# Second parts of eleven ring weights: subtraction on GpSimd instead of VectorE

## The chip, the core and the metric

The kernel runs on one core of a Trainium2 chip. The engines are TensorE (PE in the profile; its weight loads stand apart as PEld), VectorE (DVE), ScalarE (ACT), GpSimd (POOL) and SyncE (SP), which issues most of the DMAs. Each engine works through its own queue in the order written when the program is built; semaphores join them. The metric is the device time of one execution in microseconds. Before the change it is 1038.24 us, the median of three runs.

## The reference

One layer of a decoder, for a prompt of 512 tokens and eight samples of four tokens, 544 columns in all. Each layer normalises, projects, mixes in two ways in parallel (sparse attention, and a convolution), projects again, and then does a gated feed-forward block. The part that matters here is the convolution module and the input projection:

```python
def mixer_prompt(u, lp):
    q5, kv6, g3, conv_in, ga, gb = split_projection(u, lp['w_in'])
    ...
    hist = jnp.pad(conv_in, ((0, 0), (CONV_W - 1, 0), (0, 0)))
    o_conv = conformer_conv(hist, lp)
    y = merge_out(o_nsa, o_conv, ga, gb, lp['w_out'])

def conformer_conv(hist, lp):
    y = lax.conv_general_dilated(hist, lp['w_dw'][:, None, :], window_strides=(1,), padding='VALID',
                                 dimension_numbers=('NWC', 'WIO', 'NWC'),
                                 feature_group_count=C_CONV) + lp['b_dw']
    y = jax.nn.silu(layer_norm(y, lp['ln_conv_g'], lp['ln_conv_b']))
    return jnp.einsum('btc,cd->btd', y, lp['w_pw2'])
```

`split_projection` multiplies the normalised input by `w_in` (1024 rows); its columns are the queries, six key and value blocks, the branch gates, the gated conv input (`glu`) and the two merge gates. The convolution is depthwise: 31 taps on each of 512 channels, then a layer norm over the channels.

## The kernel before

**Two-part products.** The kernel keeps fp32 accuracy on TensorE by splitting each operand into two parts of a reduced fp32 form (`F32R`): a first part `h`, which ScalarE makes by a copy (`hi`, line 168), and a second part `l = raw - h`, which is a subtraction of two SBUF tensors (`lo`, line 171, on VectorE unless an engine is given). `zmm` multiplies a weight tile of 128 output columns: 16 matmuls with the first part `wh` (against both parts `hh` and `hl` of the input), and then 8 with the second part `wl`. A tile is done in two halves of 272 columns (`zhalf`, `ztile`), each with 24 matmuls; so `wl` is needed 16 matmuls after `wh`.

**The ring.** All weights stream through one ordered list, `RING`. Each entry has a time on the program's clock, a kind and a number: `(76.104, "kv", 0)`. The clock is a sorting key by which the body emits its work (an event heap, `ev`, `spawn`, `run`); it is not the time on the chip. In the stretch of the change the entries are `glu` (projection for the conv input), `kv` (twelve tiles of keys and values), `g` (branch gates), and between them `ada` and `qs` entries, which TensorE uses as they are loaded (`is_raw`). The raw weights of 512 KB go into tile `wraw`, of which there are three buffers (`NB`), and every second `ada` entry from 17 on into `xraw`, which has one. `load_more` emits a load as soon as the program's count has a buffer for it; on the chip SP's DMA waits until the last reader of the buffer it takes is done: the matmuls for a raw entry, `hi` and `lo` for a split one. SP issues loads in the planned order, so a load that waits holds those behind it.

**Splitting.** `split_upto` makes `wh` and `wl` of an entry; there are two buffers of each. `take` splits the entry that is asked for and, if it is near, the next one too. `ada_part` and `q_sample` call `split_upto` after a raw entry, so that the following tile is ready ahead of its matmuls.

**VectorE's other work there.** `conv` (line 685 on) runs the depthwise convolution, one `scalar_tensor_tensor` of 128x512 per tap (line 711), for four channel groups of 31 taps. The samples' taps are one product on GpSimd (`cpr`, line 702) and a reduction on VectorE (line 703). `layer_norm` first sends the conv state out by two DMAs of GpSimd (lines 715 and 716), adds the four groups (`lacc`, lines 719 to 721) and has TensorE sum over the channels; the products for `pw2` follow. The gated conv input `hist` and `hst` is written by VectorE (lines 678 to 682), and GpSimd's product and its output DMAs wait for that.

**The order.** The body's emission order gives the priority of each instruction. The framework then plans the order on each engine, and the buffer of each tile, with modelled costs, when the program is built; the chip follows that order.

**ScalarE around kv 7.** ScalarE's queue holds, in this order, the first part of kv 7 (line 168), a copy of keys out of PSUM (line 781), the copies for the compressed blocks (`Xc`, line 824) and `qz` (line 905), from which TensorE makes the samples' queries.

Of the kernel before, what the change touches and what calls it, by code (L numbers as in the profile page):

```python
# [79 lines left out]
def _plan():  # L80

    p = [(1 + 0.1 * n, "glu", n) for n in range(NG)]
    p += [(2.345 + 0.089 * n, "ada", n) for n in range(8, 12)]
    p += [(45.047 + 6.5 * (n - NG), "glu", n) for n in range(NG, 8)]
    p += [(76.104 + 10.023 * n, "kv", n) for n in range(12)]
    p += [(60.955 + 4.999 * n, "ada", 16 + n) for n in range(16)]
    p += [(at(3, 1.557 + 0.388 * n), "ada", 32 + n) for n in range(16)]
    p += [(164.548, "g", 0)]
    p += [(203.02 + 3.438 * n, "pw2", n) for n in range(8)]
    p += [(114.735 + 9.994 * n, "qs", n) for n in range(8)]  # L90
    p += [(TA + 6.676 * n, "q", n) for n in range(2)]
    for g in range(4):
        if g < 3:
            p += [(at(g, 6.173 if g == 0 else 5.336), "q", 2 * g + 2), (at(g, 9.783) - 1.608, "q", 2 * g + 3)]
        p += [(at(g, 12.132 + 0.267 * n) if g < 3 else at(3, 0.308 + 0.745 * n), "ga", 2 * g + n) for n in range(2)]
    for n, (g, x) in enumerate(((0, 1.6), (0, 3.4), (0, 4.8), (0, 8.0), (1, 4.5), (1, 7.7), (2, 4.5), (2, 7.7))):
        p += [(at(g, x), "gb", n)]
    p += [(TO + 3.069 * n, "out0", n) for n in range(8)]
    p += [(TO + 31.9 + 2.718 * n, "out1", n) for n in range(5)]
    p += [(TO + 50.404 + 3 * NF * hf + 2.986 * n, "fi%d" % hf, n) for hf in range(2) for n in range(NF)]  # L100
    p += [(TS + 0.008 * n, "sf", n) for n in range(NF, 44)]
    p += [(TG + 64.062 * hf + 7.662 * ft + 3.08 * kg, "fo%d" % hf, fo_entry(ft, kg))
          for hf in range(2) for ft in range(8) for kg in range(3)]
    return [(t + 1e-4 * i, kind, n) for i, (t, kind, n) in enumerate(sorted(p))]


RING = _plan()
# [5 lines left out]
def body(ctx, tc, xT, cT, cst, sel, vecs, b1row, wall, w1, pool_rows, kwin, vwin, convst, ptab,  # L113
# [53 lines left out]
    def hi(dst, src, scale=1.0):  # L167
        act.activation(dst, src, AF.Copy, scale=scale)  # L168

    def lo(dst, src, h, eng=None):  # L170
        (eng or dve).tensor_sub(dst, src, h.bitcast(F32))  # L171
# [17 lines left out]


    NB = 3
    def is_raw(j):
        _, kind, n = RING[j]
        return kind in ("ada", "qs", "sf") or kind == "glu" and n < NG
# [22 lines left out]
    def load_more(end=len(RING)):  # L217

        while rst["load"] < end:
            j = rst["load"]  # L220
            _, kind, n = RING[j]
            own = kind == "ada" and 15 < n < 32 and n % 2
            pl, tag, bufs = (xr, "xraw", 1) if own else (wp, "wraw", NB)
            if j < 4 + NG and j % 3:
# [19 lines left out]
    def split_upto(i):  # L244
        while rst["split"] <= min(i, len(RING) - 1):
            j = rst["split"]
            rst["split"] = j + 1
            if is_raw(j):
                continue
            raw, k, tag = raws.pop(j)  # L250
            out[tag] -= 1
            own = RING[j][1] == "out0" and RING[j][2] in KEPT
            h, l = ((kp if own else wp).tile([128, 1024], F32R, name=w, tag=w, bufs=3 if own else 2) for w in ("wh", "wl"))
            hi(h[:, :k], raw[:, :k])
            m = 640 if RING[j][1] in () else k
            lo(l[:, :m], raw[:, :m], h[:, :m])
            if m < k:
                lo(l[:, m:k], raw[:, m:k], h[:, m:k], pool)
            splits[j] = h.rearrange("p (k m) -> p k m", m=128), l.rearrange("p (k m) -> p k m", m=128)

    def take(kind, n):

        i = rst["use"]
        rst["use"] = i + 1
        assert RING[i][1:] == (kind, n), (RING[i], kind, n)
        if is_raw(i):
            return raws.pop(i)[::2]
        split_upto(i)
        j = i + 1
        while j < len(RING) and is_raw(j):  # L270
            j += 1
        if j - i <= NB - 1:
            split_upto(j)
        load_more()
        return splits.pop(i)
# [63 lines left out]
    def ada_part(part, bank):  # L339

        def step(k):
            raw, tag = take("ada", 8 * part + k)
            if k == 0:
                ada_ps[part] = bank()
            ada_product(ada_ps[part], k, raw)
            raw_done(tag)
            split_upto(rst["use"])
            if k == 7:
                z = ada_quarters(ada_ps.pop(part))
                ev(when("ada", 8 * part + 7) + 4.968, turn, z)  # L350

        def turn(z):
            dve.tensor_add(adaT[:, part].rearrange("p (q a) b -> p a q b", a=2), ada_turned(z)[1],
                           ada_bias(part)[:, :, :, None].to_broadcast([128, 2, 4, 9]))

        for k in range(8):
            ev(when("ada", 8 * part + k), step, k)
# [115 lines left out]
    with tc.tile_pool(name="p0", bufs=1) as p0:  # L473
# [44 lines left out]
        for f in range(NG):  # L518
            h = p0.tile([128, 8, 128], F32R, name="w0h", tag="w0h", bufs=NG)
            l = p0.tile([128, 8, 128], F32R, name="w0l", tag="w0l", bufs=NG)  # L520
            w0s.append((h, l))
            raw, tag = take("glu", f)
            raw = raw.rearrange("p (k m) -> p k m", k=8)
# [1038 lines left out]
    raw, split, bank, keep = {}, {}, {}, {}  # L1562
# [273 lines left out]
```

## Time and profile before

| what | us |
| --- | --- |
| median of three runs | 1038.24 |
| lowest and highest of them | 1037.79, 1039.67 |
| the profiled execution's own time | 1035.17 |
| its span, first to last instruction | 1033.3 |
| PE busy in it | 1006.7 |
| VectorE busy | 730.8 |
| ScalarE busy | 529.4 |
| GpSimd busy | 130.8 |

The profile is of one execution. A row of the timeline gives start, length, engine, line, operation, output and inputs, shapes and a count; in brackets stands how long the engine was idle before it and what ended that. A row of the chain of waits gives start, length and the instruction that the end of the program hung on. A window row gives the busy time of each engine in a stretch, then the granted TensorE clock, the DMA engines' busy share and the rate in GB/s. A wait row gives who waited for whom, the total, how often, and the longest. Times in rows are counted from the first instruction.

### The profile page before, as it was taken

The numbers are of one execution on the slowest core, as the hardware profiler recorded it, in microseconds if no ns is written. First come the engines' busy times: TensorE is split into PE (matmuls) and PEld (weight loads), VectorE is DVE, ScalarE is ACT, GpSimd is POOL, SyncE is SP. The second block draws the span as 40 slices with busy tenths as digits, with TensorE's granted clock in tenths as the row PEclk, the third lists the DMA queues.
The fourth block names the chain that finished last, engine by engine and source line by source line (L and its number), as shares of the span: only waits on it lengthen the run. The fifth ranks groups of instructions, "written<-read, shape, count | busy, mean of one in ns | idle before, by whom it ended". The sixth has DMA issues, their size and how long they took to land.

```text
span 1033.3 us, 21219 instructions
## 1 busy us (share of the span) xinstructions
PE 1006.7 (97%) x8488; PEld 908.3 (88%) x8488; DVE 730.8 (71%) x1356; ACT 529.4 (51%) x1174; POOL 130.8 (13%) x142
## 2 busy tenths in 40 slices
PE   9998999999999999999998999999999999999996
PEld 7898899999877777777874799999999999999996
DVE  5689996343675775766757748899888988544554
ACT  5332125465546456454535556756666666444442
POOL 0040100001244244243231000000000000000000
PEclk9999999999999999999999999999999999999998
DMA  9955865424344343424436454654323233555652
GB/s 353 392 162 198 286 196 175 146 79 142 140 144 161 106 144 125 161 83 157 150 124 203 144 209 134 219 165 142 112 93 104 101 101 105 210 175 183 203 177 84
DMA packets 52195, 167.57 MB, mean 162 GB/s; under 512 B 6224, under 2 KB 8672, under 8 KB 51712
## 3 DMA queue, kind: packets, MB, share of 16 engines
q1 hardware_dynamic: 41328, 131.38, 38.0%
q10 hardware_dynamic: 7056, 20.81, 5.6%
q0 software_dynamic: 3712, 14.02, 4.1%
q8 instruction: 67, 1.10, 0.4%
q14 instruction: 32, 0.26, 0.1%
HBM read 149.38 MB, written 16.81 MB: 161 GB/s over the span
## 4 chain that ended last, share of the span: by engine, by line
PE 84%; DMA 6%; DVE 5%; ACT 2%; issue 1%; SPq 0%; DVEq 0%; ACTq 0%
PE mm L165 51%; PE pv L165 11%; PE big L165 10%; PE pt L165 5%; DMA wraw<-in_wall_dram 4%; PE big L1138 3%; DVE cy L711 2%; PE big L609 1%; DMA first<-in_wall_dram 1%; DMA xraw<-in_wall_dram 1%; DVE wl L171 1%; PE mm L609 1%; DMA x<-in_xT_dram 1%; ACT Xc L824 1%; PE pv L538 0%
## 5 line engine op out<-in xcount | busy, mean ns | idle before, releaser
L171 DVE TENSOR_TENSOR wl<-wraw,wh 128x1024 fp32r<-128x1024 f32 (+1 forms) x135 | 156.3, 1159 | 130.8 <-ACT wh L168 116.3
L168 ACT ACTIVATE wh<-wraw 128x1024 fp32r<-128x1024 f32 (+1 forms) x183 | 166.0, 908 | 155.8 <-PE mm L165 94.3
L165 PE MATMUL mm<-hh,wh 128*128 128x272 f32 (+1 forms) x608 | 172.7, 311 | 0.5 <-ACT at L671 0.5
L165 PE MATMUL mm<-hl,wh 128*128 128x272 f32 (+1 forms) x608 | 167.4, 302 | 0.0
L165 PEld LDWEIGHTS mm<-hh,wh 128*128 128x128 f32 x608 | 116.1, 191 | 12.9 <-issue 5.9
L165 PEld LDWEIGHTS mm<-hl,wh 128*128 128x128 f32 x608 | 115.6, 190 | 5.8 <-issue 2.8
L165 PE MATMUL mm<-hh,wl 128*128 128x272 f32 (+1 forms) x608 | 100.4, 302 | 2.7 <-DVE wl L171 2.7
L165 PEld LDWEIGHTS mm<-hh,wl 128*128 128x128 f32 x608 | 85.4, 189 | 8.6 <-issue 3.0
L1110 ACT ACTIVATE PB<-big,mx 128x128 f32<-128x128 f32 (+3 forms) x128 | 66.1, 526 | 51.0 <-DVE mx L1107 45.9
L165 PE MATMUL mm<-uh,wh 128*128 128x272 f32 x352 | 90.2, 289 | 1.0 <-ACT wh L168 1.0
L165 PE MATMUL mm<-ul,wh 128*128 128x272 f32 x352 | 90.1, 288 | 0.0
L711 DVE SCALAR_TENSOR_TENSOR cy<-hist,vc,cy 128x512 f32<-128x512 f32 x120 | 88.6, 791 | 0.4
L165 PE MATMUL mm<-h2h,wh 128*128 128x272 f32 x328 | 77.4, 288 | 0.0
L1118 POOL TENSOR_SCALAR PB<-PB,mx 128x128 f32<-128x128 f32 (+3 forms) x56 | 60.7, 1099 | 78.2 <-DVE mx L1115 34.1
L165 PEld LDWEIGHTS mm<-uh,wh 128*128 128x128 f32 x352 | 66.4, 189 | 1.2 <-ACT wh L168 1.2
L165 PE MATMUL mm<-h2l,wh 128*128 128x272 f32 x260 | 66.6, 287 | 0.0
L165 PEld LDWEIGHTS mm<-ul,wh 128*128 128x128 f32 x352 | 66.2, 188 | 0.0
L165 PEld LDWEIGHTS mm<-h2h,wh 128*128 128x128 f32 x328 | 58.5, 188 | 0.0
L165 PE MATMUL mm<-h2h,wl 128*128 128x272 f32 x312 | 53.1, 288 | 0.5 <-ACT pv L1605 0.5
L165 PE MATMUL mm<-uh,wl 128*128 128x272 f32 x352 | 52.2, 288 | 0.0
L1107 DVE TENSOR_REDUCE mx<-big 128x2 f32<-128x256 f32 (+3 forms) x64 | 51.0, 816 | 0.5
L165 PEld LDWEIGHTS mm<-h2l,wh 128*128 128x128 f32 x260 | 48.9, 188 | 0.0
(489 smaller groups left out, 2212.0 us busy)
## 6 DMA issues: line engine op xcount, KB each, us to landing
wraw<-in_wall_dram SPq DMA_DIRECT2D x170, 512.0 KB, 4.2
X<-in_rows_dram SPq DMA_DIRECT2D x32, 256.0 KB, 5.0
wraw<-in_wall_dram SPq DMA_DIRECT2D x16, 384.0 KB, 3.7
first<-in_wall_dram SPq DMA_DIRECT2D x8, 512.0 KB, 10.2
xraw<-in_wall_dram SPq DMA_DIRECT2D x8, 512.0 KB, 6.5
kw<-in_kwin_dram ACTq DMA_DIRECT2D x8, 512.0 KB, 3.5
out_wk_dram<-kw ACTq DMA_DIRECT2D x8, 512.0 KB, 5.2
vw<-in_vwin_dram ACTq DMA_DIRECT2D x8, 512.0 KB, 3.5
```

The source lines that it names most:

```text
L165: pe.matmul(out, lhsT, rhs, start=start, stop=stop, **more)
L168: act.activation(dst, src, AF.Copy, scale=scale)
L171: (eng or dve).tensor_sub(dst, src, h.bitcast(F32))
L609: ins = pe.matmul(gl[f][hf][:, :HT], w[:, k], r[:, k, sl], start=k == 0 and part == 0, stop=k == 7 and part == 2).ins
L711: dve.scalar_tensor_tensor(y, hist[:, ct, k:k + TP], w, y, op0=OP.mult, op1=OP.add)
L824: act.activation(o, src[:, r], AF.Copy)
L1107: dve.tensor_reduce(mx[:, 0, r, 2 * jj:2 * jj + 2], sc[:, :, :w], axis=AX.X, op=OP.max, negate=True)
L1110: act.activation(P[r][:, :, j * 128:j * 128 + 128], sc[:, jp, :w].rearrange("p (k n) -> p k n", n=128), AF.Exp, bias=mx[:, 0, r, j:j + 1], ...
L1118: (dve if r or g == 3 and i > 1 else pool).tensor_scalar(v, v, m[:, j:j + 1], None, op0=OP.mult)
L1138: pe.transpose(p[:, x, j * 128:j * 128 + 128], P[r][:, kt, j * 128:j * 128 + 128], ident)
```

## The change

The second part of a ring weight whose clock lies strictly between 68 and 165 is worked out by GpSimd, all 1024 columns of it. The entries are glu 7, kv 0 to 8 and g; raw entries have no second part. All other weights keep VectorE. The first parts, the matmuls and the loads are written as they were.

```diff
@@ -189,6 +189,8 @@
     NB = 3
+    A_LO, B_LO = 68, 165
+
     def is_raw(j):
@@ -252,8 +254,9 @@
             hi(h[:, :k], raw[:, :k])
-            m = 640 if RING[j][1] in () else k
-            lo(l[:, :m], raw[:, :m], h[:, :m])
+            m = 0 if A_LO < RING[j][0] < B_LO else k
+            if m:
+                lo(l[:, :m], raw[:, :m], h[:, :m])
             if m < k:
                 lo(l[:, m:k], raw[:, m:k], h[:, m:k], pool)
```

## The prediction

> **What bounds the kernel now.** I read the page first, then the groups of the moved line, the waits of PE, the chain of waits in the stretch of the change, and the timelines of POOL, ACT and PE there.
>
> ```profile
> span 1033.3 us, 21219 instructions
> PE 1006.7 (97%) x8488; PEld 908.3 (88%) x8488; DVE 730.8 (71%) x1356; ACT 529.4 (51%) x1174; POOL 130.8 (13%) x142
> 86.00:112.00 26.00, 26.00 (x227) 23.62 (x227) 26.00 (x35) 5.01 (x12) 3.88 (x4) 1.00 0.67 222
> 170.00:190.00 20.00, 19.93 (x182) 18.68 (x181) 5.03 (x6) 13.48 (x35) 0.00 (x0) 1.00 0.46 160
> ```
>
> TensorE is busy for 97% of the span. In the windows (columns: stretch, length, then busy time of PE, PEld, DVE, ACT, POOL) both PE and DVE are full from 86 to 112 us; from 170 to 190 PE still is (19.93 of 20) and DVE is three quarters idle. Two full engines side by side do not say which one sets the end. The moved line does:
>
> ```profile
> L171 DVE TENSOR_TENSOR wl<-wraw,wh x11: 1205/1226/1226, 89.5 to 182.7; 128x1024 fp32r<-128x1024 f32 x11
> its engine sat idle before it (us, times) until:
>   ACT wh L168: 8.8, 6
> who waited for it (us, times):
> ```
>
> ```profile
> PE mm L165 <- DVE wl L171: 2.7, 1, 2.7
> 118.73 0.64 PE L165 MATMUL big<-xraw,cs 128*32 128x256 f32 x8 [1.84 <-DMA xraw<-in_wall_dram]
> 82.11 1.21 DVE L171 TENSOR_TENSOR wl<-wraw,wh 128x1024 fp32r<-128x1024 f32 x1
> ```
>
> The change moves eleven ring entries: glu 7 (clock 71.05), kv 0 to 8 (76.1 to 156.3) and g (164.55). In the order of the ring they are these eleven subtractions, from 89.5 to 182.7 us, and under "who waited" stands nothing: no compute engine waited for any of them. The second fence has PE's wait on a `wl` and two timeline rows. Between 60 and 240 us PE waits on a `wl` once, for 2.7 us, and that one runs at 82.11 us. It belongs to glu 6, whose clock is 64.55, below 68; it stays on VectorE, and all that stands ahead of it is unchanged. So VectorE is relieved where PE does not wait for it.
>
> Someone else does wait for these subtractions: the next load. A `wraw` buffer is free only when the subtraction has read it, and SP issues the next DMA then.
>
> ```profile
> SPq L236 <- DVE wl L171: 21.7, 8, 5.9
> SPq L236 <- PE big L165: 18.3, 9, 7.1
> 160.25 1.07 ACT wh L168
> 161.34 1.24 DVE wl L171
> 163.01 6.12 DMA wraw<-in_wall_dram
> 169.22 1.06 ACT wh L168
> 178.78 0.29 ACT qz L905
> 179.12 0.41 PE pt L165 x2
> ```
>
> The first two rows are SP's waits between 84 and 190 us, for VectorE and for PE; the others are the chain of waits. In this stretch the chain leaves PE: ScalarE's first part of kv 6 (160.25), its second part on VectorE (161.34), the load issued by SP behind that (163.01), the first part of kv 7 (169.22), then ScalarE's queue without a pause until `qz` at 178.78, ended at 179.07, and `qz`'s product on PE at 179.12. PE idles for 0.07 us in these twenty (above), so it was done just as `qz` was: its slack there is under 0.1 us, I take 0.05, and what is late on this chain is late on PE.
>
> **The change part by part.** Removed from VectorE: 11 x 1.21 us = 13.3 us, and nothing of the span, because nobody on PE waits. Added on GpSimd: 11 subtractions of 128x1024 with both inputs in SBUF. The trace has none of that form; the nearest rows are these:
>
> ```profile
> L702 POOL TENSOR_TENSOR cpr<-hst,vc 128x992 f32<-128x992 f32 x4 | 9.9, 2487 | 21.5 <-issue 14.6 <-DVE cy L703 5.4 <-DMA hst<-in_conv_dram 1.6
> L1020 POOL TENSOR_TENSOR m<-m,O 128x272 f32<-128x272 f32 x6 | 4.6, 774 | 15.0 <-DVE O L1018 8.4 <-DVE mx L1115 6.6
> 83.87 2.56 POOL L702 TENSOR_TENSOR cpr<-hst,vc 128x992 f32<-128x992 f32 x1 [14.58 <-issue]
> 83.67 3.31 DVE L711 SCALAR_TENSOR_TENSOR cy<-hist,vc,cy 128x512 f32<-128x512 f32 x2
> 150.29 6.71 DVE L711 SCALAR_TENSOR_TENSOR cy<-hist,vc,cy 128x512 f32<-128x512 f32 x10
> ```
>
> The product at line 702 is almost the same size and runs beside conv taps: 2.49 us, times 1024/992 = 2.57 us. I take 2.55 us. The upper end is the sum of line 1020 in proportion, 774 ns x 1024/272 = 2.9 us; the lower one is the time for which VectorE is held (next paragraph), 2.0 us.
>
> The last three rows show what GpSimd costs VectorE. Ten taps alone take 6.71 us, 0.67 each; the two taps beside GpSimd's product take 3.31 instead of 1.34 us, 1.97 more. So each move takes 1.14 us off VectorE (1.21 less the overlap with the next start) and puts some 1.9 us back as blocked time: VectorE gets not shorter but 0.75 us longer per entry. After glu 7 and kv 0 to 3 it is about 3.8 us late, and then it stays so, since its pauses before the six later subtractions (8.8 us, above) go too.
>
> The Trainium skill, GPSIMD Engine Reference, section "3.1 Elementwise — side-by-side cycle accounting", gives 4497 ns for such an operation at 2048 elements; half of it, as an estimate, is 2.25 us, and with it the sum below would be +1.7 instead of +2.5 us.
>
> VectorE's lateness costs nothing as long as the layer norm has room:
>
> ```profile
> 168.77 0.72 DVE L721 TENSOR_TENSOR lacc<-lacc,cy 128x544 f32<-128x544 f32 x1
> 189.47 0.62 PE L165 MATMUL pt<-lacc,c 128*128 128x272 f32 x2
> ```
>
> The last sum after the taps ends at 169.5, its product stands at 189.5 in PE's order. That room of 20 us is also why a faster VectorE could win nothing. Its price if the room were gone is up to 3.8 us.
>
> Now the path that sets the end, the loads behind kv 4 to kv 7:
>
> ```profile
> 149.95 0.22 PE big L165 x4
> 148.06 1.06 ACT L168 ACTIVATE wh<-wraw 128x1024 fp32r<-128x1024 f32 x1 [4.55 <-DMA wraw<-in_wall_dram]
> 149.15 1.23 DVE L171 TENSOR_TENSOR wl<-wraw,wh 128x1024 fp32r<-128x1024 f32 x1 [1.22 <-ACT wh L168]
> 150.41 0.84 SPq L236 DMA_DIRECT2D wraw<-in_wall_dram  x2
> 153.08 1.18 PE L165 MATMUL mm<-hh,wl 128*128 128x272 f32 x8
> 162.42 0.39 PE L165 MATMUL mm<-hh,wh 128*128 128x272 f32 x1
> 164.54 1.18 PE L165 MATMUL mm<-hh,wl 128*128 128x272 f32 x8
> ```
>
> From kv 4 on VectorE stands idle when the first part is done, so the second part ends 1.26 us after it (148.06 + 1.06 to 150.38); on GpSimd 2.55: +1.3 us each time, and each time SP's next burst of four loads starts behind it, in order.
> - kv 4: its burst's first load is 1.3 us later, but the later ones wait for PE anyway (9 such waits, above) and follow at SP's pace of 0.4 us: kv 5's load, the fourth, lands between +0.4 (one step of SP) and +1.3; I take +0.7.
> - kv 5: 0.7 + 1.3 = +2.0. Its second part is ready at 152.4, needed at 153.08: no wait. But the burst of 150.41 starts 2.0 us later, and kv 6's first part is ready at 163.3 instead of 161.3, needed at 162.42: PE waits about 0.9.
> - kv 6: +3.3 us; its second part is ready at 165.9, with PE at 164.54 + 0.9: 0.4 us more. The burst behind it starts 3.3 us later, and so do kv 7's first part and ScalarE's queue up to `qz`. PE loses 3.3 in all at 179 us (the 1.3 already lost is within it).
> - Against this, kv 3's second part no longer stands behind conv taps (below): -0.2.
>
> ```profile
> 112.15 1.17 PE L165 MATMUL mm<-hh,wl 128*128 128x272 f32 x8
> 126.00 1.06 ACT L168 ACTIVATE wh<-wraw 128x1024 fp32r<-128x1024 f32 x1 [1.46 <-DMA wraw<-in_wall_dram]
> 128.63 1.21 DVE L171 TENSOR_TENSOR wl<-wraw,wh 128x1024 fp32r<-128x1024 f32 x1
> 107.69 2.23 POOL L702 TENSOR_TENSOR cpr<-hst,vc 128x992 f32<-128x992 f32 x1
> ```
>
> The second part of kv 3 ends at 129.84 now, on GpSimd at 127.06 + 2.55 = 129.6. Here VectorE's queue cost as much as GpSimd's slowness; for glu 7 and kv 0 to 2 it cost more, but their buffers' next loads, or the tiles themselves, are not what PE waits for.
>
> A gain is possible at PE's 1.8 us wait for `xraw` at 118.73. VectorE, 2.3 us later by then, lets GpSimd's last conv product (107.69) and its two output transfers, issued just ahead of it and behind it, start later, outside that load's flight. Between 0 and 1.8 us; I take 0.5, near nothing, because the load was released by PE itself.
>
> **Sum:** +3.3 - 0.2 - 0.05 (slack) - 0.5 = +2.5 us. Its own time of 1035.17 (span 1033.3 and 1.9 around it) becomes 1037.7. That execution was 3.1 us below the median of 1038.24, so I give 1038.24 + 2.5 = 1040.7. From 179 us on PE is full and the later waits follow it, so the loss is kept.
>
> **The rivals.**
>
> *Loads take other buffers.* The order on every engine and the buffer of every load are planned when the program is built, with GpSimd's price in the plan. If the plan sees PE free a buffer (ada and qs entries) before GpSimd does, the burst starts behind PE, as early as today or 0.5 us earlier, and the loop costs nothing. For it: the product of an ada entry ends at 150.17 (149.95 + 0.22), 0.2 us before the second part of kv 5. Against it: ScalarE's order shows the plan has the loads landing earlier than they do. Then -0.5 to -1.5: 1037.2 us.
>
> *Faster, by the clock.* The wait at 118.73 is followed by this:
>
> ```profile
> 116.00:119.40 3.40, 1.56 (x20) 0.52 (x18) 3.40 (x5) 0.40 (x1) 0.00 (x0) 1.00 1.03 401
> 119.40:122.80 3.40, 3.40 (x15) 3.40 (x16) 3.40 (x7) 0.38 (x1) 0.00 (x0) 0.50 1.01 295
> 78.44:81.85 3.41, 2.25 (x20) 2.02 (x16) 3.41 (x7) 0.00 (x0) 0.00 (x0) 1.00 0.59 165
> ```
>
> After 3.4 us with PE busy for 1.56 the granted clock was 0.50 for 3.4 us, a loss of 1.7; with 2.25 busy it stayed at 1.00. If the wait shrinks enough, both go: -1.8 - 1.7 = -3.5, 1034.7 us. It decides only together with the first rival, else the chain of loads holds the time anyway.
>
> *Slower, by the clock.* The new wait of some 2 us before 179 us falls into one such stretch: +1.7, 1042.4 us. The Trainium skill, TensorE: Matmul & The Clock Gate, "Part 1: The HAM clock gate", has a free-running window of about 3.4 us; by that rule it hangs on where the window's edge lies; the stretch of 119.40 at 0.50, 3.4 us long, agrees.
>
> *GpSimd's queue.* kv 1's subtraction is planned behind the last conv product and the output DMAs, which wait for VectorE (the product ends at 109.9 today, some 2.3 us later with the change): ready near 115, PE needs it at 112.15 (the eight matmuls above). PE loses 3 there and about 3 by the late load behind it: +6, 1044.2 us. Against it: its first part is done before VectorE writes what those need.
>
> **How the numbers follow.** Forecast 0.42 (its own range 1038.1 to 1042.3: with 2.0 us per subtraction and the whole 1.8 gained, 0.4 + 0.75 + 0.75 - 0.25 - 1.8 = -0.15; with 2.9 and nothing gained, 1.0 + 1.65 + 1.65 - 0.25 = +4.05), other buffers 0.24, faster by the clock 0.13, slower by the clock 0.13, queue 0.08. What this kernel's measurement can tell from no change is 0.2%, 2.1 us. Slower: 0.27 of the forecast's share, 0.13 and 0.08: 0.48. Same: the forecast's other 0.15 and 0.21 of the other buffers: 0.36. Faster: 0.13 and 0.03. The range is 1035.2 to 1044.0; it leaves out the end of each clock and queue case.
>
> **What would show it.** Right: eleven POOL rows of 2.2 to 2.7 us, taps beside them stretched to about 2.6, kv 5 to kv 7 first parts 0.7, 2 and 3.3 us later against PE, a PE wait near 179. Wrong: bursts released by PE instead of POOL, or no half clock at 119 us; or a much longer POOL row.

## The result, and the profile after

| | median us | runs | from, to |
|---|---|---|---|
| before | 1038.01 | 4 | 1037.67, 1039.67 |
| after | 1052.82 | 4 | 1048.33, 1054.49 |

The changed kernel takes 1.0134 times as long, 95% interval 1.0113 to 1.0154. The profiled execution took 1048.33 us, its span is 1046.6, 13.3 more than before. It is the fastest of the four: the others took 1052.03 to 1054.49 us at a mean granted clock of 0.986 to 0.988 in place of 0.992, and the rows below account for the 13.3 alone. Where they went is read first from PE's idle time. The windows from 60 to 240 us (columns as in the prediction), before:

```profile
60.00:240.00 180.00, 174.96 (x1580) 164.12 (x1579) 132.72 (x202) 67.26 (x151) 11.19 (x10) 0.99 0.51 169
```

and after, followed by the stretch of half clock that is there now:

```profile
60.00:240.00 180.00, 163.63 (x1479) 151.47 (x1478) 128.65 (x187) 61.43 (x138) 50.04 (x18) 0.98 0.48 162
132.85:139.68 6.83, 3.15 (x14) 3.15 (x15) 6.83 (x10) 0.40 (x1) 3.63 (x1) 0.50 0.23 77
```

PE is idle for 16.4 us of these 180, where it was for 5.0: 11.3 of the 13.3 us are here. Of the other 2.0, 1.8 are PE's busy time, 1008.5 us in the whole span in place of 1006.7; what lengthens it isn't settled. In this execution the half clock is not a second loss: its stretch is twice as long, but PE works in only 3.15 of its 6.83 us, which costs 1.6 us, as much as the stretch at 119.40 before, in which PE worked for all of 3.40 us (1.7). PE's waits in the same 180 us, after:

```profile
PE mm L165 <- POOL wl L171: 7.8, 3, 7.2
PE mm L165 <- DVE wl L171: 2.9, 1, 2.9
PE mm L165 <- ACT wh L168: 2.0, 2, 1.4
PE pt L165 <- ACT qz L908: 1.4, 1, 1.4
PE big L165 <- DMA xraw<-in_wall_dram: 1.3, 2, 0.9
```

The first row is new: PE waits for GpSimd's `wl`, 7.2 us of it at one place. GpSimd's own timeline (start, duration, what ended the idle time before) shows which:

```profile
85.64 2.81 POOL L171 TENSOR_TENSOR wl<-wraw,wh 128x1024 fp32r<-128x1024 f32 x1
96.47 8.04 POOL L171 TENSOR_TENSOR wl<-wraw,wh 128x1024 fp32r<-128x1024 f32 x2 [8.01 <-ACT wh L168]
...
114.34 2.89 POOL L171 TENSOR_TENSOR wl<-wraw,wh 128x1024 fp32r<-128x1024 f32 x1
127.12 9.36 POOL L171 TENSOR_TENSOR wl<-wraw,wh 128x1024 fp32r<-128x1024 f32 x1 [9.90 <-ACT wh L168]
141.41 2.49 POOL L171 TENSOR_TENSOR wl<-wraw,wh 128x1024 fp32r<-128x1024 f32 x1 [4.93 <-ACT wh L168]
156.06 5.18 POOL L171 TENSOR_TENSOR wl<-wraw,wh 128x1024 fp32r<-128x1024 f32 x1 [12.16 <-ACT wh L168]
171.47 2.38 POOL L171 TENSOR_TENSOR wl<-wraw,wh 128x1024 fp32r<-128x1024 f32 x1 [10.22 <-ACT wh L168]
```

All of one shape, and yet 2.38 to 9.36 us (the row at 96.47 holds two, kv 0 and kv 1). The long one is kv 3. What VectorE did in its time:

```profile
126.25 8.03 DVE L714 SCALAR_TENSOR_TENSOR cy<-hist,vc,cy 128x512 f32<-128x512 f32 x12
134.20 0.22 DVE L356 TENSOR_TENSOR adaT<-pt,vc 128x72 f32<-128x72 f32 x1
134.34 7.32 DVE L714 SCALAR_TENSOR_TENSOR cy<-hist,vc,cy 128x512 f32<-128x512 f32 x8
```

Twelve conv taps in 8.03 us are 0.67 each: unhindered, although GpSimd's subtraction stands there from 127.12. Then comes the adaT sum (VectorE adds the bias to a product of the `ada` entries, 72 columns read from PSUM), and the eight taps behind it take 7.32 us in place of 5.4: there GpSimd has got in, and ends at 136.48. A row's duration therefore holds two things, a wait to begin and some 2.4 us of work. PE's row follows at once:

```profile
136.53 1.73 PE L165 MATMUL mm<-hh,wl 128*128 128x272 f32 x6 [7.18 <-POOL wl L171]
```

The same stretch of VectorE before, for later:

```profile
125.83 2.72 DVE L711 SCALAR_TENSOR_TENSOR cy<-hist,vc,cy 128x512 f32<-128x512 f32 x4
128.48 0.21 DVE L353 TENSOR_TENSOR adaT<-pt,vc 128x72 f32<-128x72 f32 x1
```

In that run four taps stood ahead of the sum, now twelve do. Counted over the whole convolution it is 85 taps in place of 78 (by the rows of the second execution below; the profile shown here lacks one tap's record). So where four subtractions have left VectorE's queue ahead of the sum (4 x 1.14 = 4.6 us), the planned order has seven more taps (7 x 0.66 = 4.6 us). The sum starts 5.7 us later. What makes it late are the taps beside GpSimd's subtractions: those at 87.25, 99.37, 102.18 and 115.99 us last 1.75, 2.89, 2.88 and 1.78 us in place of 0.74, 6.3 us more in all.

### The profile page after: what moved, and what is told of

Its sections match the earlier page's. It is cut to its first block, busy times and chain, and to the rows that moved or that the text cites. A ratio compares the mean times of both kernels' runs of the same rounds, so it can differ in the third digit from the quotient of the medians.

```text
span 1046.6 us, 21218 instructions
## 1 busy us (share of the span) xinstructions
PE 1008.5 (96%) x8488; PEld 908.3 (87%) x8488; DVE 729.8 (70%) x1345; ACT 529.3 (51%) x1174; POOL 170.2 (16%) x153
## 4 chain that ended last, share of the span: by engine, by line
PE 79%; DMA 8%; DVE 5%; ACT 3%; POOL 2%; issue 1%; SPq 1%; another core or an unknown queue 0%; ACTq 0%; DVEq 0%
PE mm L165 47%; PE big L165 11%; PE pv L165 10%; DMA wraw<-in_wall_dram 6%; PE pt L165 5%; PE big L1141 3%; POOL wl L171 2%; DVE cy L714 1%; DMA xraw<-in_wall_dram 1%; ACT PB L1113 1%; ACT wh L168 1%; DVE wl L171 1%; DMA X<-in_rows_dram 1%; ACT Xc L827 1%; PE pt L541 0%
## 5 line engine op out<-in xcount | busy, mean ns | idle before, releaser
L171 DVE TENSOR_TENSOR wl<-wraw,wh 128x1024 fp32r<-128x1024 f32 (+2 forms) x124 | 142.9, 1154 | 130.6 <-ACT wh L168 114.9
L714 DVE SCALAR_TENSOR_TENSOR cy<-hist,vc,cy 128x512 f32<-128x512 f32 x120 | 100.8, 897 | 0.3
L171 POOL TENSOR_TENSOR wl<-wraw,wh 128x1024 fp32r<-128x1024 f32 x11 | 40.2, 3655 | 61.3 <-ACT wh L168 53.0
```

What stands on the lines that cost most here:

```text
L714: dve.scalar_tensor_tensor(y, hist[:, ct, k:k + TP], w, y, op0=OP.mult, op1=OP.add)
```

## The experiments

Theory **shut out**: while VectorE runs taps one behind another, GpSimd's subtraction cannot begin. Rivals: **late buffers**, the prediction's reason (each subtraction ends 1.3 us later and the loads behind it with it); **slow operation** (the duration varies on GpSimd by itself); and later **VectorE late** (what VectorE still does comes too late). In the diffs, `-` is the changed kernel.

**The same kernel again.**

> The changed kernel a second time. Theory 'shut out': a subtraction on GpSimd cannot begin while VectorE runs conv taps one behind another, and gets in when another instruction breaks the run of taps. Then the four rows without taps beside them (kv 6, kv 7, kv 8, g) are again 2.3 to 2.5 us, the rows beside taps again lie anywhere between 2.4 and 9.4 us, and in each long one several taps of the usual 0.74 us lie before one stretched to 2.6 to 2.9 us. Which row is long may differ; if kv 3's is short, the time falls by about 8 us. Theory 'late buffers' (the prediction's): the long row is an accident of one execution, nearly all rows are 2.4 to 2.9 us and the loss stays. Theory 'slow operation' (GpSimd's subtraction varies by itself): long rows also among the last four.

It took 1049.31 us. GpSimd's timeline, kv 3 to kv 5:

```profile
129.05 2.46 POOL L171 TENSOR_TENSOR wl<-wraw,wh 128x1024 fp32r<-128x1024 f32 x1 [10.21 <-ACT wh L168]
137.34 4.63 POOL L171 TENSOR_TENSOR wl<-wraw,wh 128x1024 fp32r<-128x1024 f32 x1 [5.83 <-ACT wh L168]
152.01 12.55 POOL L171 TENSOR_TENSOR wl<-wraw,wh 128x1024 fp32r<-128x1024 f32 x1 [10.04 <-ACT wh L168]
```

kv 3 is short now, and kv 5 takes 12.55 us, after which PE has waited 9.9. So the time did not fall by 8 us, as expected for a short kv 3: another entry was caught. The four without taps beside them are again 2.38 to 2.40. For kv 3 it hung on the moment at which its subtraction came up. VectorE's first tap of a channel group (line 712, one input) in the first execution and in this one:

```profile
125.79 0.54 DVE L712 TENSOR_SCALAR cy<-hist,vc 128x512 f32<-128x512 f32 x1
129.17 2.62 DVE L712 TENSOR_SCALAR cy<-hist,vc 128x512 f32<-128x512 f32 x1
```

Here kv 3 came up at 129.05, just ahead of it, and got in there; in the first execution it came up at 127.12, behind it, and had to wait for the adaT sum.

**kv 3 alone on GpSimd.**

```diff
-            m = 0 if A_LO < RING[j][0] < B_LO else k
+            m = 0 if RING[j][1:] == ("kv", 3) else k
```

> Only kv 3's second part on GpSimd, the other ten on VectorE. Shut out: VectorE is not late here, so kv 3's subtraction comes up at about 127.1 us with two or three taps ahead of the adaT sum (128.5 us in the kernel before), where it gets in: its row is 2.5 to 4.5 us, it ends at 129.6 to 131.6 us against 129.84 before, and the time is within 0 to +2.5 us of the kernel before. Late buffers: one entry of the loop, ready 0.2 us earlier to 0.3 us later: -0.3 to +0.5 us. Slow operation (kv 3's own place or buffers make it slow): its row is again some 9 us, and +9 to +13 us.

Ratio to before 1.0003 (0.9987 to 1.0019). VectorE kept its old order, four taps ahead of the adaT sum, which came at 128.94 us; the subtraction stood there from 128.69 and got in:

```profile
128.69 2.57 POOL L171 TENSOR_TENSOR wl<-wraw,wh 128x1024 fp32r<-128x1024 f32 x1 [17.82 <-ACT wh L168]
```

The entry is not slow by itself: slow operation loses, and the other two both allow this.

**kv 4 to g alone.**

```diff
-    A_LO, B_LO = 68, 165
+    A_LO, B_LO = 110, 165
```

> Only kv 4 to kv 8 and g on GpSimd (lower bound of the clock 110 in place of 68); everything up to kv 3 is as before. Late buffers: the whole chain of the prediction's sum from kv 4 to kv 7 is in this half: +2.5 us, rows of 2.4 to 2.9 us. Shut out: kv 4's subtraction comes up at about 136.5 us in a run of 36 taps that lasts from 129.8 to about 153.6 us; if it gets in at the first change of taps, +1 to +4 us; if not, its row is as long as the run, up to 17 us, and the time up to 15 us more. kv 6 to g without taps beside them: 2.3 to 2.5 us. Slow operation: long rows anywhere.

Six moved entries cost more than eleven: ratio 1.018 (1.015 to 1.021). The expectation had put the worst case at 15 us; it was 18.6. GpSimd's row of kv 4, the run of taps beside it, and PE's wait:

```profile
136.86 19.31 POOL L171 TENSOR_TENSOR wl<-wraw,wh 128x1024 fp32r<-128x1024 f32 x1 [26.83 <-ACT wh L168]
```

```profile
129.40 23.93 DVE L714 SCALAR_TENSOR_TENSOR cy<-hist,vc,cy 128x512 f32<-128x512 f32 x36
153.25 0.71 DVE L722 TENSOR_TENSOR lacc<-cy 128x544 f32<-128x544 f32 x1
```

```profile
156.22 2.18 PE L165 MATMUL mm<-hh,wl 128*128 128x272 f32 x8 [14.33 <-POOL wl L171]
```

36 taps in 23.93 us, not one of them stretched, and GpSimd waiting from 136.86 to the end of the run. Of the 18.6 us this wait makes up 14.3. Late buffers had +2.5 us here.

**A memset between the taps.** This leaves all eleven on GpSimd and gives VectorE more to do.

```diff
     cy = cp.tile([128, 4, T], F32, name="cy")
+    brk = cp.tile([128, 1], F32, name="brk")
...
                 dve.scalar_tensor_tensor(y, hist[:, ct, k:k + TP], w, y, op0=OP.mult, op1=OP.add)
+            dve.memset(brk, 0.0)
```

> The changed kernel with a memset of one column on VectorE after each conv tap (124 of them; the order puts some of the first ones together, from 95 us on they alternate with the taps). Shut out: each GpSimd row is at most one tap's rest and 2.4 us, 2.4 to 3.2 us; PE's wait of 7.2 us at kv 3's second part falls to 0 to 1.5 us, the half clock there to at most 3.4 us; the kernel gets 6 to 10 us faster than the changed one (1048.3): +2 to +6 us against the kernel before, though VectorE has more work. Late buffers or a late VectorE: the memsets make VectorE later, so the time is that of the changed kernel or up to 5 us more: +13 to +18 us. Slow operation: rows of 5 to 9 us remain.

Ratio to before 1.0043 (1.0027 to 1.0058). The subtractions by line (minimum, median, maximum in ns, first and last start) and the taps at kv 3:

```profile
L171 POOL TENSOR_TENSOR wl<-wraw,wh x11: 2372/2503/2854, 86.8 to 188.0; 128x1024 fp32r<-128x1024 f32 x11
```

```profile
127.75 0.74 DVE L715 SCALAR_TENSOR_TENSOR cy<-hist,vc,cy 128x512 f32<-128x512 f32 x1
127.76 0.06 DVE L716 MEMSET brk<- 128x1 f32 x1
128.42 2.95 DVE L715 SCALAR_TENSOR_TENSOR cy<-hist,vc,cy 128x512 f32<-128x512 f32 x1
128.43 0.06 DVE L716 MEMSET brk<- 128x1 f32 x1
```

No row is over 2.85 us, GpSimd gets in at the next tap, and of 1.34% there are 0.43% left. Late buffers and a late VectorE both had the time of the changed kernel or more. VectorE is not earlier here: its adaT sum starts at 135.80 us, and PE waits for a `wl` of GpSimd's 0.2 us in all. The planned order differs a little, with 80 taps ahead of that sum.

**The memset alone**, with no entry moved, the control:

```diff
-    A_LO, B_LO = 68, 165
+    A_LO, B_LO = 0, 0
```

> The kernel before (no entry on GpSimd) with the memset after each conv tap: the cost of the memsets by themselves, the control for the runs that have them. 53 memsets stand between taps, and a tap with one follows the last after 0.67 in place of 0.66 us: VectorE some 1 us later at the end of the taps, where it has 20 us of room: 0 to +0.5 us. If the order of the taps changes by it, up to 2 us either way.

1.0002 (0.9986 to 1.0017): no cost that these runs can tell from nothing.

**kv 4 to g with the memset.**

```diff
-    A_LO, B_LO = 68, 165
+    A_LO, B_LO = 110, 165
```

> Only kv 4 to kv 8 and g on GpSimd, as in the run that was 1.8% slower, now with the memset after each conv tap. Shut out: kv 4's row falls from 19.3 to at most 3.2 us, PE's wait of 14.3 us goes, and the time falls by 14 to 18 us; what is left is the late buffers' part, the prediction's +2.5 us (+1.5 to +4.5 with half clock) against the kernel before. Late buffers alone: the time stays where it was, +18 us.

1.0004 (0.9992 to 1.0016), where it was 1.018: one column of zeros is worth 18 us. Late buffers' +2.5 is outside the interval too, though its waits are in the trace, PE's between 60 and 240 us:

```profile
PE pt L165 <- ACT qz L910: 1.4, 1, 1.4
PE mm L165 <- ACT wh L168: 1.2, 2, 0.6
```

In the control, PE waits 1.2 us for the adaT sum near 176 us and has 3.4 us of half clock behind it; that wait is not in this list. Whether one took the other's place isn't settled.

**kv 6 to g alone, where no taps are**, without the memset: the late buffers by themselves.

```diff
-    A_LO, B_LO = 68, 165
+    A_LO, B_LO = 130, 165
```

> Only kv 6, kv 7, kv 8 and g on GpSimd (lower bound of the clock 130): no conv taps beside them, so nothing shuts them out and VectorE is not blocked: four rows of 2.3 to 2.5 us. What is left is the late buffers' part alone: kv 6's second part ends 1.2 us later (2.4 against 1.2), the burst of loads behind it starts 1.2 us later, kv 7's first part and ScalarE's queue up to qz too, and PE waits up to 1.2 us more there. The prediction's way of counting gives +1.2 us against the kernel before; if loads or ScalarE have room, 0.

1.0026 (1.0010 to 1.0042), +1.0 to +4.4 us. The rows are 2.37 to 2.66 us, and PE waits for `qz` at 182 us, as the prediction's chain has it:

```profile
PE pt L165 <- ACT qz L908: 1.4, 1, 1.4
```

The mechanism is there, and its size for one entry, 1.2, lies within the interval.

**glu 7 to kv 2 alone**, without the memset.

```diff
-    A_LO, B_LO = 68, 165
+    A_LO, B_LO = 68, 100
```

> Only glu 7 and kv 0 to kv 2 on GpSimd (upper bound of the clock 100); kv 3 and all later ones on VectorE. VectorE late: the four blocked stretches put the adaT sum some 5 us later than before (134.2 against 128.5 us in the changed kernel), and kv 3's second part, which stands behind it in VectorE's order, too: PE waits 4 to 6 us there, and with half clock and late loads +6 to +12 us. Shut out alone: no second part that PE waits for is on GpSimd, and a shut-out GpSimd does not block VectorE: 0 to +2 us. Late buffers: kv 0 to kv 2 have room: 0 to +0.5 us.

1.0099 (1.0073 to 1.0124), with no `wl` that PE waits for on GpSimd. VectorE's timeline and PE's wait:

```profile
129.67 8.02 DVE L714 SCALAR_TENSOR_TENSOR cy<-hist,vc,cy 128x512 f32<-128x512 f32 x12
137.62 0.22 DVE L356 TENSOR_TENSOR adaT<-pt,vc 128x72 f32<-128x72 f32 x1
137.76 1.20 DVE L171 TENSOR_TENSOR wl<-wraw,wh 128x1024 fp32r<-128x1024 f32 x1
```

```profile
139.02 2.18 PE L165 MATMUL mm<-hh,wl 128*128 128x272 f32 x8 [8.95 <-DVE wl L171]
```

VectorE late: twelve taps are planned ahead of the adaT sum and kv 3's second part behind it. In the changed kernel this second part is on GpSimd, so there the same lateness is not paid in this way.

**Only glu 6, with the memset**: the one second part for which PE waited before.

```diff
-    A_LO, B_LO = 68, 165
+    A_LO, B_LO = 64, 65
```

> Only glu 6 on GpSimd (bounds 64 and 65: the one second part that PE waits for in the kernel before, 2.7 us), with the memset after each conv tap. Its first part ends at 76.3 us, VectorE takes it up at 82.1 only. Shut out, mended by the memset: the subtraction runs from 76.3 to at most 80.2 us, PE's wait of 2.7 us shrinks to 0 to 0.5, and the time is 2 to 3 us below the kernel before (1.7 more where the half clock that follows this wait in some runs goes too); the memsets cost VectorE about 0.01 us each. If the memset does not help, the row ends at 82.5 us and 0 to 1 us is won. Late buffers: PE is ahead of the loads by then, nothing is won: -0.5 to +0.5 us.

1.0011 (0.9995 to 1.0027): nothing won, where shut out had expected 2 to 3 us. GpSimd ran it at 77.64 us in 2.62, and the wait of 2.7 is gone (0.2 is left, for a later `wl` of VectorE's), but the next one, for a load (1.8 before), grew:

```profile
PE big L165 <- DMA xraw<-in_wall_dram: 3.1, 1, 3.1
```

**Three probes.** What in the run of taps does it? The layer is taken away; VectorE runs taps in place, and GpSimd's subtraction is released by ScalarE at moments some 0.05 us apart (0.11 in the third probe). The core of the first:

```python
    def tap(y, n=512):
        dve.scalar_tensor_tensor(y[:, :n], hist[:, :n], w, y[:, :n], op0=OP.mult, op1=OP.add)
...
        for k in range(14):
            tap(cy[0])
        pool.tensor_sub(wl, raw, h)
```

> The layer is left out and zeros are written to every output. In its place stand 68 trials, one behind another: GpSimd does one subtraction of 128x1024 (the last 12: the conv product of 128x992), released by ScalarE at a moment that shifts by about 0.07 us from trial to trial, while VectorE runs 14 instructions back to back. Each kind has a line of its own. Shut out: alone (line 152) 2.4 us; beside taps added into one accumulator (line 157) a mixture of about 2.4 to 3.1 us and of rows that last until the run of taps ends, 8 to 10 us, mean over 5; beside taps with a memset between (163) at most 3.2 us, mean 2.8; beside one-input instructions (178) 2.4 us. Open: taps of two lengths in turn (168), taps on four accumulators in turn (173), the conv product beside taps (184). If what lets GpSimd in is that the run is irregular, 168 is short like 163; if it is an instruction that doesn't read two inputs, 168 is long like 157. If the product is privileged (8 of 8 got in at once so far), 184 is at most 3.2 us each time. Slow operation: 152 and 178 vary as much as 157. Late buffers: every kind at most 3.2 us.

This expectation failed: nothing was shut out. The groups of GpSimd by line (count, busy us, mean ns, idle before); line 157 is the subtraction beside bare taps, line 163 the same with a memset behind each tap:

```profile
L163 POOL TENSOR_TENSOR wl<-raw,wh 128x1024 fp32r<-128x1024 f32 x12 | 31.1, 2591 | 144.5 <-ACT wh L141 134.1 <-DVE cy L162 10.4
...
L157 POOL TENSOR_TENSOR wl<-raw,wh 128x1024 fp32r<-128x1024 f32 x12 | 30.6, 2548 | 119.2 <-ACT wh L141 119.2
```

But these taps, all on one accumulator, started 0.79 us apart and lasted 0.75, with 0.04 between, and the release fell into the second of them. (On four accumulators in turn, line 173, there is no gap; there the release fell into the second or third tap of the run, and GpSimd got in at the next one, 12 times of 12, with mean 2.56 us.) In the kernel the taps of two channel groups take turns and start 0.66 us apart: 0.08 before the one ahead ends. The second probe has that, with runs of 24 taps and the release in the sixth to eighth:

```python
        y = cy[k % chains]
        x = hist[:, k % chains, k:k + 512]
        dve.scalar_tensor_tensor(y, x, w, y, op0=OP.mult, op1=OP.add)
```

> The layer is left out and zeros are written to every output, as in the first probe, but closer to the kernel: runs of 24 taps, the subtraction released 3.6 to 4.4 us into the run (12 moments 0.055 us apart for each kind), taps on two accumulators in turn as in the kernel, where one starts 0.08 us before the one ahead has ended (in the first probe, which shut nothing out, the single accumulator left gaps of 0.04 us, and the four accumulators were met in the first three taps, which wait for nothing). Shut out where there is no gap: line 166 (two accumulators) and line 190 (the same with the conv product) show some rows of 2.4 to 3.1 us and some that last to the end of the run, about 12 us; line 171 (four accumulators) too; line 161 (one accumulator, gaps) at most 3.2 us; line 177 (a memset after each tap) at most 3.2 us; line 184 (a memset after each sixth) at most 6.5 us. Shut out by something else in the kernel (PE, ScalarE or DMA traffic): every line at most 3.2 us.

```profile
L166 POOL TENSOR_TENSOR wl<-raw,wh 128x1024 fp32r<-128x1024 f32 x12 | 162.8, 13566 | 72.8 <-ACT wh L146 67.7 <-DVE cy L151 5.1
L171 POOL TENSOR_TENSOR wl<-raw,wh 128x1024 fp32r<-128x1024 f32 x12 | 162.8, 13566 | 59.6 <-ACT wh L146 54.5 <-DVE cy L151 5.1
L190 POOL TENSOR_TENSOR cpr<-hst,dw 128x992 f32<-128x992 f32 x12 | 160.1, 13340 | 70.1 <-ACT hst L146 65.0 <-DVE cy L151 5.1
...
L177 POOL TENSOR_TENSOR wl<-raw,wh 128x1024 fp32r<-128x1024 f32 x12 | 30.8, 2568 | 183.5 <-ACT wh L146 151.1 <-DVE brk L176 32.5
L161 POOL TENSOR_TENSOR wl<-raw,wh 128x1024 fp32r<-128x1024 f32 x12 | 30.2, 2514 | 215.6 <-ACT wh L146 177.5 <-DVE cy L151 38.2
```

With two accumulators (166), with four (171) and with the conv product (190), GpSimd waits out the run in all 36 trials, mean 13.3 to 13.6 us; with one (161) or with the memset (177) in none. So, for a release this far into the run, it is no matter of chance or of which GpSimd operation, and it needs no work of PE or of the DMAs beside it. What goes with it is the missing gap. (In line 184, with a memset behind each sixth tap, the release fell close behind the first memset, and GpSimd got in at the next tap, 12 times of 12; in five of them a tap had begun between the memset and the release.)

The third probe puts one other instruction behind the twelfth of 24 taps:

> The layer is left out and zeros are written to every output, as in the second probe: runs of 24 taps on two accumulators in turn, the subtraction released some 4 us into the run (6 moments for each kind). After the twelfth tap, 8.0 us into the run, stands one other instruction of VectorE, a kind for each line; if it lets GpSimd in, the row is 8.0 - 4 + 2.4 = some 6 to 7 us, if not, it is 13 to 14 us as in the second probe. 166: a memset of one column. 173: a tap on a third accumulator. 180: a two-input instruction of 272 columns on a third accumulator (like the hist product, after which kv 0's got in). 187: a second tap on the same accumulator, which has to wait for the one ahead. 194: a one-input instruction of 512 columns. 201: the same of 32 columns. 208: a two-input one that reads PSUM (like the adaT sum, after which kv 3's got in). If only a gap or an instruction that does not read two SBUF inputs lets it in: 166, 187, 194, 201 and 208 some 6.5 us, 173 and 180 some 13.5. If any change of the instruction does: all some 6.5. If only a gap does: 187 alone.

```profile
L173 POOL TENSOR_TENSOR wl<-raw,wh 128x1024 fp32r<-128x1024 f32 x6 | 85.5, 14255 | 37.5 <-ACT wh L149 32.4 <-DVE cy L154 5.1
L180 POOL TENSOR_TENSOR wl<-raw,wh 128x1024 fp32r<-128x1024 f32 x6 | 84.0, 14004 | 29.6 <-ACT wh L149 24.5 <-DVE cy L154 5.1
L194 POOL TENSOR_TENSOR wl<-raw,wh 128x1024 fp32r<-128x1024 f32 x6 | 83.9, 13988 | 30.2 <-ACT wh L149 25.1 <-DVE cy L154 5.1
...
L166 POOL TENSOR_TENSOR wl<-raw,wh 128x1024 fp32r<-128x1024 f32 x6 | 34.0, 5663 | 73.4 <-ACT wh L149 60.4 <-DVE cy L154 13.0
L201 POOL TENSOR_TENSOR wl<-raw,wh 128x1024 fp32r<-128x1024 f32 x6 | 33.9, 5658 | 69.9 <-ACT wh L149 56.7 <-DVE cy L154 13.2
L208 POOL TENSOR_TENSOR wl<-raw,wh 128x1024 fp32r<-128x1024 f32 x6 | 33.9, 5642 | 77.2 <-ACT wh L149 64.2 <-DVE cy L154 13.0
```

None of the three answers foreseen: the memset (166), the one-input instruction of 32 columns (201) and the 72 columns from PSUM (208) let GpSimd in, six times of six; a tap on a third accumulator (173), a two-input instruction of 272 columns (180) and the one-input one of 512 (194) do not. Among these kinds the short ones let it in and the long ones do not, whatever the number of inputs. In 187 the second tap on the same accumulator was ordered to the end of the run:

```profile
L187 POOL TENSOR_TENSOR wl<-raw,wh 128x1024 fp32r<-128x1024 f32 x6 | 81.8, 13627 | 32.7 <-ACT wh L149 27.0 <-DVE cy L154 5.7
```

It starts 0.04 us after the tap ahead has ended (at 370.30 us in the first trial), the only gap of the run, and lasts 2.71 us, six times of six: GpSimd, kept out until then, got in at the first gap.

## Why the prediction was wrong, by its own steps

- **The direction** was right, with slower given the best chance; the size, +2.5, was not: +14.8 by the medians.
- **The step that failed** is GpSimd's duration: "I take 2.55 us", with 2.0 and 2.9 as its ends. As work this was good: 2.36 to 2.41 us without taps, 2.85 at most with the memset. But a row beside taps also holds the wait to begin, and that had no upper end but the run's: up to 9.36, 12.55 and 19.31 us. Behind it stood the reading of line 702: four products beside VectorE's conv work, 2.23 to 2.61 us, were taken as the price beside taps. They were not a sample of it: the second probe's row 190 shows the same product shut out in twelve trials of twelve. What to ask of such a row is what let it in each time.
- **kv 3's "-0.2"** (129.6 in place of 129.84) is the same failure at its place: 136.48, and 7.2 us of PE's waits hang on it.
- **"Nobody on PE waits"** for the moved `wl` was true of the profile before and became false by the wait to begin.
- **VectorE** was to be some 3.8 us late and to pay nothing, with 20 us of room. At the layer norm it is not late at all: the last sum starts at 168.65 us, 168.77 before. At the adaT sum it is 5.7 us late. The prediction set the subtractions' time free against the blocked taps there; the planned order filled that time with seven more taps, so that the blocked 6.3 us stay whole. That the room at the layer norm is not the only thing VectorE owes is shown by the run of glu 7 to kv 2: 8.95 us of wait for kv 3.
- **The chain of loads**: right in kind, and SP's waits after bear it out (84 to 200 us):

```profile
SPq L238 <- POOL wl L171: 42.2, 8, 9.7
```

  The bursts are released by GpSimd's subtraction, eight of them as VectorE's had released eight before, so the rival by which loads take other buffers falls. PE's waits from 140 to 200 us sum to 1.4 for `qz`, 0.7 for `QB`, 0.6 for `wh` and 0.6 for `wl`, 3.3 in all, as summed. That is in part luck: kv 3's lateness has shifted everything by then, and the run of kv 4 to g with the memset (+0.4, -0.8 to +1.7) gives less. The run without taps (+1.0 to +4.4) is the clean one.
- **The gain at `xraw`**: 1.8 us before, 1.3 in two waits after, 0.5 as taken; the half clock behind it went, and came back at 132.85.
- **The clock rivals**: slower by the clock was to cost 1.7 more. In the profiled execution the half clock moved and costs 1.6 us as before. Faster by the clock had its condition met at 119.40, where the half clock went, but it came back behind the wait for kv 3.
- **GpSimd's queue** falls: kv 1's subtraction ran right behind kv 0's (the pair at 96.47), ahead of the last product and its DMAs.

The Trainium skill, SBUF — State Buffer, section "Who interferes with whom", says that a VectorE instruction with two SBUF inputs contends with a GpSimd instruction that reads SBUF, that the port pair they share is an exclusive lock, and that the order of issue decides who blocks. Taps stretched to up to 2.95 us agree. Read instruction by instruction, that rule would end GpSimd's wait with the tap under way, at most 0.75 us; the runs show it lasting over a whole run without gaps, and there the measurement decides.

Of the 1.34%, shut-out makes up about 0.9: that is what the memset gives back. What makes the remaining 0.43% stays open. Late loads are one candidate, with 0.26% in the run without taps, but with the memset no wait for `qz` is in the trace; PE waits there for the second adaT sum (2.3 us near 178, 1.2 in the control) and for `wh` (1.4, 0.9 in the control). And with the memset PE idles 6.2 us between 60 and 240, in the control 5.1, which is less than the difference of the two times.

## What to carry to other kernels

Before work is moved to GpSimd beside a busy VectorE, read the starts of VectorE's two-input instructions, not only their durations: where each starts before the one ahead has ended, a GpSimd operation that reads SBUF may wait for the whole run, and an engine's row that looks slow may be one that has not begun. If the work has to stand there, break the run with something very short, such as a memset of one column, whose cost could not be told from nothing here. And an order planned by prices fills the time that an engine is thought to gain, so look at what the plan has put ahead of the things others wait for.

## What was not expected of the hardware

- Runs of 512-column taps 0.66 us apart kept GpSimd out in 36 of 36 trials in which it came up in the seventh or eighth tap; runs with gaps of 0.04 us did so in none of the 12 in which it came up in the sixth or seventh.
- One input or two does not settle it: in the probe a one-input instruction of 512 columns inside the run kept GpSimd out as well, and one of 32 columns let it in. The kernel's own one-input instruction of 512 columns (line 712) let it in, in the second execution. The Trainium skill, SBUF — State Buffer, section "Who interferes with whom", counts `tensor_scalar`, which all three are, among those that can take both ports in a mode of their own; no run here tells whether they were in that mode.
- Left open is what exactly lets GpSimd in. In the kernel it got in behind two-input instructions of 544 columns (the layer norm's sum at 153.25 in the run of kv 4 to g) and of 272 (`hist` at 99.01 in the changed kernel, for kv 0), though the probe's 272 columns did not allow it. In the changed kernel it also got in at the next tap, with no gap to be seen, for kv 4 (141.41) and for kv 1, which came up while a tap was still stretched by kv 0. In the probes it did so early in a run (lines 173 and 184). Whether the waits of an instruction leave a gap there, or the place in the run decides, wasn't tried.
